# The last gate/up pair interleaved with slim quartets, and every down-projection operand loaded as a split pair

## The chip, the cores and the metric

One core of a Trainium2 chip runs the kernel. The metric is the device time of one execution in microseconds; lower is better. Everything is computed in fp32. TensorE takes fp32 matrices only in a rounded form, so each operand is split into a high and a low part, and one block product costs three matmuls of 128x128 weights on 320 columns.

## The reference, cut to what matters

One step of a hybrid encoder layer on 640 tokens (512 of a prompt, 8 times 16 of decoding). The change touches only the feed-forward part, with `D_MODEL` 2048 and `D_FF` 5632:

```python
def merge_and_ffn(x, oa, ob, ...):
    o = jnp.concatenate([rmsnorm(oa, norm_grp_a), rmsnorm(ob, norm_grp_b)], axis=-1)
    x = x + o @ w_out
    h = rmsnorm(x, norm_ffn)
    return x + (jax.nn.silu(h @ w_gate) * (h @ w_up)) @ w_down
```

## The kernel before

**Stages.** Input projection, attention and decoding run until about 700 us, the output projection until about 857 us, then come 22 feed-forward *pairs* (of 2 times 128 rows of `w_gate` and of `w_up`) until about 1949 us, then 32 steps of the down-projection until about 2500 us, and a final norm.

**Quartets.** A 2x2 block product is done with seven products instead of eight (`quartet`, L764): p1, p6, p7, p2, p5, p4, p3, each on a sum or difference of weight blocks b11, b12, b21, b22 and of operand blocks. In a pair the gate quartet (7 products of 24 matmuls) runs, then the up quartet. A quartet of a down-projection step has 7 products of 3 matmuls for each active pair: five active pairs make 105 matmuls.

- The weight combinations: `b12 -= b22` (L797) and `s6 = b11 - b12` (L801) on VectorE, `b11 = b22 - s6` (L804) and `b21 -= s6` (L813) on GpSimd. In the gate quartet of pair 0 VectorE does the last two as well (L809, L813).
- `split` (L226, L227) makes the high part of a weight block on ScalarE and the low part on VectorE. Three products' worth of split slots (H) exist.
- The partial products are added from PSUM on VectorE (L823).

**Between gate/up and down.** `store_part` (L1168) splits one of the seven operand parts of a finished pair (ScalarE, then VectorE at L1176) and stores the two halves to DRAM (`act_d`). `START` says at which down-projection step a pair enters; pairs 0 to 4 are active in step 0. An operand is fetched split by `fetch` (L1109), a 320 KB load that GpSimd's queue issues (L1112). GpSimd works in order: a load that waits for its slot holds what stands behind it. Pairs 1, 2 and 3 (`raw_pairs`) are an exception: their parts are stored whole (`first_d`, L1240), loaded by SP as the normalized inputs `hs` come free (`free`, L1118), and split on chip by `split_raws` (L1140: ScalarE L1148 21 times, VectorE L1149 14 times, GpSimd L1149 7 times). Pair 21, the last, is never stored: its parts stay in SBUF, and `keep_last` (L1154: ScalarE L1159, VectorE and GpSimd L1160) splits them during step 0; it enters in step 1.

**The order.** The program is written in one order, and a scheduler then places each engine's instructions; `keep_turns` (L143) adds dependencies that keep the tiles of one slot in the order in which they were taken, so a slot that is taken elsewhere can move instructions of other work. Work put in `n.later` stands behind the other work on ScalarE, VectorE and GpSimd. `prepare` (L1048) makes the operand parts of `hs` in pair 0's gate quartet, one set ahead of each product (L1070 to L1075, with their own splits at L226 and L227).

Of the kernel before, what the change touches and what calls it, by code (L numbers as in the profile page):

```python
# [8 lines left out]
ALU = mybir.AluOpType  # L9
# [21 lines left out]
START = [25, 27, 28, 30, 31, 3, 4, 6, 7, 8, 9, 11, 12, 14, 15, 16, 17, 19, 20, 22, 23, 1]  # L31
# [288 lines left out]
def build(nc, tc, io, pools):  # L320
# [442 lines left out]

    def quartet(k, load, lefts, before=None, after=None, part="all", eng=nc.gpsimd):  # L764

        def product(src, which, bank):
            own = n.get("H"), n.get("H")
            hl = [r(sh(x, k, P)) for x in own]
            at = n.emitted()
            n.split(sh(src, k, P), *hl)  # L770
            n.last_split = at, n.emitted()
            if before:
                before(which)
            for j in range(k):
                n.mm3(bank, (hl[0][:, j], hl[1][:, j]), lefts[j][which][1], j == 0, j == k - 1)
            n.put("H", *own)
            if after:
                after(which)
            return bank
# [8 lines left out]
        if part == "late":  # L788
            b21, b22 = get(2), get(3)
            for name, src, which in (("p2", b21, 4), ("p3", b22, 6)):  # L790
                yield name, product(src, which, n.bank()[:, :HT])
                n.put("W", src)
            return
# [17 lines left out]
        if part == "all":  # L811
            yield "p2", product(b21, 4, n.bank()[:, :HT])
        eng.tensor_tensor(b21[:, w], b21[:, w], s6[:, w], sub)  # L813
        n.put("W", s6)
        yield "p5", product(b11, 3, x[:, 1])
        n.put("W", b11)
        yield "p4", product(b21, 5, n.bank()[:, :HT])
        n.put("W", b21)
        if part == "all":
            yield "p3", product(b22, 6, y[:, 1])  # L820
        n.put("W", b22)

# [197 lines left out]
    first_d = dram("first_d", (7, P, 3, HT))  # L1020
# [94 lines left out]
    raw_pairs = active(0)[1:4]  # L1115
    raws, late, kept, kept_own = [], [], {}, []

    def free(which):  # L1118

        n.put("S", *(h[which][0] for h in hs))  # L1120
        own = []
        for j in raw_pairs[::2]:
            k = min(2, raw_pairs[-1] + 1 - j)
            raw = n.get("S")
            dma(out=sh(raw, k, HT), in_=first_d[which, :, j - raw_pairs[0]:j - raw_pairs[0] + k])
            own.append((j, k, raw))
# [12 lines left out]

    def split_raws():  # L1140
        at = n.emitted()
        which, own = raws.pop(0)
        for j, k, raw in own:
            for a in range(k):
                t = n.get("S")
                hi, lo = hl = pack(t, HT)
                part = raw[:, a * HT:a * HT + HT]
                nc.scalar.activation(hi, part, AF.Identity)  # L1148
                (nc.vector, nc.gpsimd)[a].tensor_tensor(lo, part, f(hi), ALU.subtract)  # L1149
                lefts[j + a][which] = t, hl  # L1150
            n.put("S", raw)
        n.later.append((at, n.emitted()))
# [28 lines left out]
    gate = None  # L1181
    for i in range(NPAIR):
        for src in ("w_gate", "w_up"):
            blocks = [(2 * i, 0), (2 * i + 1, 0), (2 * i, 8), (2 * i + 1, 8)]
            load = lambda z: io[src][blocks[z][0], :, blocks[z][1]:blocks[z][1] + 8]
            y = [n.get("S")]
            c11, c21 = y[0][:, :HT], y[0][:, HT:]
            start, end = i == 0 and src == "w_gate", i == NPAIR - 1 and src == "w_up"
            for step, bank in quartet(8, load, hs, (lambda w: next(prep)) if start else None, free if end else None,
                                      eng=nc.vector if start else nc.gpsimd):  # L1190
                if step == "p1":
                    nc.scalar.activation(c11, bank, AF.Identity)
                elif step == "p6":
                    y.append(n.get("S"))
                    c12, c22 = y[1][:, :HT], y[1][:, HT:]
                    add(c12, c11, bank)
                elif step == "p7":
                    add(c21, c12, bank)
                elif step == "p5":
                    add(c22, c21, bank)  # L1200
                    add(c12, c12, bank)
                elif step == "p2":
                    add(c11, c11, bank)
                elif step == "p4":
# [255 lines left out]
```

## Time and profile before

| what | value |
|---|---|
| median of 3 runs | 2529.17 us (2527.81 to 2533.78) |
| the profiled execution: its own time, its span | 2528.33 us, 2526.6 us |
| TensorE (PE) busy | 2484.5 us, 98% of the span |
| VectorE (DVE) busy | 1965.5 us, 78% |
| ScalarE (ACT) busy | 1055.0 us, 42% |
| GpSimd (POOL) busy | 701.9 us, 28% |
| the chain that ended last | PE 88%, DVE 7%, issue 2%, DMA 2%, ACT 1% |

A matmul counts as busy until its modelled end, so a busy PE can still be late; what PE loses is seen better by counting matmuls in a stretch. A busy VectorE counts the time in which it is held up by GpSimd, too. The profiled execution was 1.7 us longer than its span, and 0.8 us below the median.

### The profile page before, as it was taken

To read this page: it belongs to the slowest core of one execution; us is meant where nothing else is said; L and a number is where in the kernel's file an instruction comes from. 1 tells how busy PE (TensorE), PEld (TensorE's weight loads), DVE (VectorE), ACT (ScalarE), POOL (GpSimd) and SP (SyncE) were. 2 spreads that over 40 slices of the span, in tenths; PEclk is the share of its full clock that TensorE was granted. 3 is DMA by queue.
4 is the path that set the end of the run, shared out by engine and by line. 5 is a ranking of instruction groups with operands and counts; after the bars stand their busy time and mean duration, and the time that the engine had idled before them with its cause. 6 is when DMAs were issued, how large, how long until landed. Compare 5 with 4: busy or idle time off the path is not lost.

```text
span 2526.6 us, 44669 instructions
## 1 busy us (share of the span) xinstructions
PE 2484.5 (98%) x17325; PEld 2420.7 (96%) x17325; DVE 1965.5 (78%) x2930; ACT 1055.0 (42%) x1701; POOL 701.9 (28%) x566
## 2 busy tenths in 40 slices
PE   8999999999999999999999999999999999999997
PEld 8998999987799999999999999999999999999997
DVE  6657766685668887788888888888889877777797
ACT  5446333365555543343343343434434333333343
POOL 1001212110022043323333232333325433333453
PEclk9999999999999999999999999999999999999998
DMA  6233433478664434543344334334437756666655
GB/s 198 83 97 119 163 132 119 147 248 292 229 201 145 148 112 147 166 148 121 124 145 136 128 129 150 120 123 146 132 127 259 234 167 177 176 170 178 181 161 183
DMA packets 191605, 401.68 MB, mean 159 GB/s; under 512 B 22497, under 2 KB 83937, under 8 KB 191393
## 3 DMA queue, kind: packets, MB, share of 16 engines
q1 hardware_dynamic: 167056, 344.75, 41.8%
q0 software_dynamic: 23184, 52.77, 7.6%
q8 instruction: 136, 2.23, 0.4%
q10 hardware_dynamic: 1152, 1.31, 0.2%
q14 instruction: 77, 0.62, 0.1%
HBM read 311.14 MB, written 86.87 MB: 158 GB/s over the span
## 4 chain that ended last, share of the span: by engine, by line
PE 88%; DVE 7%; issue 2%; DMA 2%; ACT 1%; SPq 0%; POOL 0%; DVEq 0%; ACTq 0%; POOLq 0%
PE dn L235 18%; PE dn L237 18%; PE dn L236 17%; PE at L235 10%; PE at L237 10%; PE at L236 10%; DVE W L227 2%; PE at L341 2%; PE at L464 1%; PE at L425 1%; DVE S L823 1%; DMA W<-w_in 1%; PE at L743 0%; DMA W<-xT 0%; ACT S L438 0%
## 5 line engine op out<-in xcount | busy, mean ns | idle before, releaser
L226 ACT ACTIVATE W<-W 128x1024 fp32r<-128x1024 f32 (+2 forms) x662 | 640.3, 968 | 1064.3 <-PE dn L236 582.4
L235 PE MATMUL dn<-S,W 128*128 128x320 f32 x3374 | 1054.5, 313 | 7.4 <-ACT S L1159 3.8
L237 PE MATMUL dn<-S,W 128*128 128x320 f32 x3374 | 1045.8, 310 | 5.7 <-DVE W L227 5.4
L236 PE MATMUL dn<-S,W 128*128 128x320 f32 x3374 | 1044.2, 309 | 0.3 <-DVE S L227 0.3
L227 DVE TENSOR_TENSOR W<-W,W 128x1024 fp32r<-128x1024 f32 (+2 forms) x662 | 800.3, 1209 | 90.5 <-ACT W L226 83.2
L235 PEld LDWEIGHTS dn<-S,W 128*128 128x128 f32 x3374 | 634.3, 188 | 22.3 <-issue 13.5
L237 PEld LDWEIGHTS dn<-S,W 128*128 128x128 f32 x3374 | 633.6, 188 | 11.6 <-DVE W L227 9.9
L236 PEld LDWEIGHTS dn<-S,W 128*128 128x128 f32 x3374 | 634.4, 188 | 0.8 <-DVE S L227 0.6
L237 PE MATMUL at<-S,W 128*128 128x320 f32 x1834 | 567.8, 310 | 1.0 <-DVE W L227 1.0
L235 PE MATMUL at<-S,W 128*128 128x320 f32 x1834 | 567.9, 310 | 0.5 <-ACT W L226 0.5
L236 PE MATMUL at<-S,W 128*128 128x320 f32 x1834 | 567.7, 310 | 0.0
L804 POOL TENSOR_TENSOR W<-W,W 128x1024 f32<-128x1024 f32 (+2 forms) x84 | 181.4, 2159 | 772.9 <-DVE W L227 629.1
L237 PEld LDWEIGHTS at<-S,W 128*128 128x128 f32 x1834 | 345.1, 188 | 1.7 <-DVE W L227 1.4
L235 PEld LDWEIGHTS at<-S,W 128*128 128x128 f32 x1834 | 345.1, 188 | 0.7 <-ACT W L226 0.7
L236 PEld LDWEIGHTS at<-S,W 128*128 128x128 f32 x1834 | 345.1, 188 | 0.0
L823 DVE TENSOR_TENSOR S<-S,dn 128x320 f32<-128x320 f32 x398 | 182.5, 482 | 80.0 <-PE dn L237 79.7
L813 POOL TENSOR_TENSOR W<-W,W 128x1024 f32<-128x1024 f32 (+2 forms) x84 | 186.1, 2216 | 183.7 <-DVE W L227 132.8
L823 DVE TENSOR_TENSOR S<-S,at 128x320 f32<-128x320 f32 x292 | 138.6, 484 | 96.5 <-PE at L237 94.8
L797 DVE TENSOR_TENSOR W<-W,W 128x1024 f32<-128x1024 f32 (+2 forms) x86 | 117.4, 1365 | 40.8 <-DMA W<-w_gate 29.4
L801 DVE TENSOR_TENSOR W<-W,W 128x1024 f32<-128x1024 f32 (+2 forms) x86 | 95.9, 1115 | 55.1 <-DMA W<-w_up 29.6
L1112 POOL DMA_DIRECT2D S<-act_d x161 | 88.0, 547 | 166.5 <-PE dn L237 80.0
L1176 DVE TENSOR_TENSOR S<-S,half 128x320 fp32r<-128x320 f32 x147 | 120.3, 839 | 1.9
(157 smaller groups left out, 1700.4 us busy)
## 6 DMA issues: line engine op xcount, KB each, us to landing
S<-act_d POOLq DMA_DIRECT2D x161, 320.0 KB, 3.8
W<-w_gate SPq DMA_DIRECT2D x88, 512.0 KB
W<-w_up SPq DMA_DIRECT2D x88, 512.0 KB
W<-w_in SPq DMA_DIRECT2D x66, 512.0 KB
W<-w_down SPq DMA_DIRECT2D x64, 384.0 KB
act_d<-half SPq DMA_DIRECT2D x147, 160.0 KB
act_d<-S SPq DMA_DIRECT2D x147, 160.0 KB
W<-w_down SPq DMA_DIRECT2D x68, 320.0 KB
```

What stands on the lines that cost most here:

```text
L226: self.nc.scalar.activation(hi, src, AF.Identity)
L227: self.nc.vector.tensor_tensor(lo, src, f(hi), ALU.subtract)
L235: mm(out, a[0], b[0], start=first, stop=False)
L236: mm(out, a[0], b[1], start=False, stop=False)
L237: mm(out, a[1], b[0], start=False, stop=last)
L797: nc.vector.tensor_tensor(b12[:, w], b12[:, w], b22[:, w], sub)
L801: nc.vector.tensor_tensor(s6[:, w], b11[:, w], b12[:, w], sub)
L804: eng.tensor_tensor(b11[:, w], b22[:, w], s6[:, w], sub)
L813: eng.tensor_tensor(b21[:, w], b21[:, w], s6[:, w], sub)
L823: add = lambda o, a, b: nc.vector.tensor_tensor(o, a, b, ALU.add)
L1112: nc.gpsimd.dma_start(out=r(sh(t, 2, HT)), in_=r(act_d[which, :, j]))
L1176: nc.vector.tensor_tensor(r(src), src, hi, ALU.subtract)
```

## The change

- **The last pair.** `product` is taken out of `quartet`, and `slim_quartet` does the same seven products in the order p1, p7, p6, p5, p3, p2, p4 with three weight slots instead of four (b12 is worked on in place). `slim_collect` adds up the results with single PSUM tiles (one VectorE add more in each quartet). Gate and up of pair 21 run product by product in turns, 14 products, so the seven `free` calls come two products apart, over both quartets.
- **Operands.** `first_d`, `raw_pairs` and `split_raws` are gone: pairs 1 to 3 are stored by `store_part` like the others (21 ScalarE and 21 VectorE splits, 42 stores of 160 KB in place of 21), and all five pairs of step 0 are fetched from `act_d` by GpSimd: 35 loads of 320 KB instead of 14 (and SP's `first_d` loads go, 3.4 MB).
- **Pair 21** enters in step 3 instead of 1, pair 5 in step 1 instead of 3 (`START`). Its `activate` and `products` run as later work in steps 0 and 1, `keep_last` in step 2.
- `load_sums`: the loads of the residual for a step are issued one step earlier.
- The gate/up loop uses `collect` for all pairs; the first result slot is therefore taken when p1 is done and no longer ahead of the quartet.

```diff
-START = [25, 27, 28, 30, 31, 3, 4, 6, 7, 8, 9, 11, 12, 14, 15, 16, 17, 19, 20, 22, 23, 1]
+START = [25, 27, 28, 30, 31, 1, 4, 6, 7, 8, 9, 11, 12, 14, 15, 16, 17, 19, 20, 22, 23, 3]
...
+    def slim_quartet(k, load, lefts, after=None):
...
+        b11, b12, b22 = get(0), get(1), get(3)
+        nc.vector.tensor_tensor(b12[:, w], b12[:, w], b22[:, w], sub)
+        yield "p1", multiply(b11, 0)
+        yield "p7", multiply(b12, 2)
+        nc.vector.tensor_tensor(b12[:, w], b11[:, w], b12[:, w], sub)
+        nc.gpsimd.tensor_tensor(b11[:, w], b22[:, w], b12[:, w], sub)
+        yield "p6", multiply(b12, 1)
+        yield "p5", multiply(b11, 3)
+        n.put("W", b11)
+        b21 = get(2)
+        yield "p3", multiply(b22, 6)
+        n.put("W", b22)
+        yield "p2", multiply(b21, 4)
+        nc.gpsimd.tensor_tensor(b21[:, w], b21[:, w], b12[:, w], sub)
+        n.put("W", b12)
+        yield "p4", multiply(b21, 5)
+        n.put("W", b21)
...
     def free(which):
 
         n.put("S", *(h[which][0] for h in hs))
-        own = []
-        for j in raw_pairs[::2]:
...
         fetch_late()
-        raws.append((which, own))
         late.append(which)
-        if len(raws) > 2:
-            split_raws()
 
     def fetch_late():
         for which in late:
             for j in active(0):
-                if j not in raw_pairs:
-                    fetch(j, which)
+                fetch(j, which)
         late.clear()
...
-            y = [n.get("S")]
-            c11, c21 = y[0][:, :HT], y[0][:, HT:]
...
+    both = [slim_collect(slim_quartet(8, weights_of(NPAIR - 1, src), hs, after))
+            for src, after in (("w_gate", None), ("w_up", free))]
+    ys = [None, None]
+    for z in range(14):
+        ys[z % 2] = next(both[z % 2])
+        if z and z % 2 == 0:
+            store_part()
...
             if t == 0:
                 fetch_late()
-                if which in (1, 2):
-                    split_raws()
+            if (t == 0 and which in (2, 3)) or (t == 1 and which in (0, 2, 3)):
+                at = n.emitted()
+                next(finish_last, None)
+                n.later.append((at, n.emitted()))
+            elif t == 2:
                 for x in {0: (0,), 2: (1,), 4: (2,), 3: (4,), 5: (3,), 6: (5, 6)}.get(which, ()):
                     keep_last(x)
...
-        if t < 8:
-            x, y = n.get("S"), n.get("S")
...
+        if t == 0:
+            load_sums(0)
...
+                if t < 7:
+                    load_sums(t + 1)
```

GpSimd at the start of the down-projection, before. L804 and L813 are the weight combinations of step 0, L1149 and L1160 splits of operand parts, L1112 the fetches, L1231 and L1233 parts of pair 21's products:

```order
L804 TENSOR_TENSOR W_3036_20719<-W_3035_20717,W_3037_20722 128x640
L1149 TENSOR_TENSOR S_3046_20775<-S_3013_20638,S_3046_20775 128x320
L1231 TENSOR_TENSOR S_2930_20121<-S_2962_20381 128x320
L1112 DMA S_3139_21292<-act_d 128x640
L1112 DMA S_3113_21160<-act_d 128x640
L1149 TENSOR_TENSOR S_3052_20805<-S_3022_20684,S_3052_20805 128x320
L1112 DMA S_3128_21255<-act_d 128x640
L1112 DMA S_3146_21339<-act_d 128x640
L1233 TENSOR_TENSOR S_2941_20191<-S_2979_20463,S_2941_20191 128x320
L1160 TENSOR_TENSOR S_3054_20811<-S_2941_20191,S_3054_20811 128x320
L1112 DMA S_3151_21365<-act_d 128x640
L813 TENSOR_TENSOR W_3055_20816<-W_3055_20816,W_3037_20722 128x640
```

The same place after (L806 and L815 are now the combinations of step 0, L1142 the fetches, L1190 the end of the silu of pair 21):

```order
L1142 DMA S_3048_20762<-act_d 128x640
L806 TENSOR_TENSOR W_3027_20652<-W_3026_20650,W_3028_20655 128x640
L1142 DMA S_3051_20788<-act_d 128x640
L1142 DMA S_3055_20812<-act_d 128x640
L1142 DMA S_3058_20834<-act_d 128x640
L1142 DMA S_3067_20868<-act_d 128x640
L1142 DMA S_3070_20892<-act_d 128x640
L815 TENSOR_TENSOR W_3044_20740<-W_3044_20740,W_3028_20655 128x640
L1190 TENSOR_TENSOR S_2936_20135<-S_2936_20135,S_1716_9931 128x640
L1142 DMA S_3134_21272<-act_d 128x640
L1190 TENSOR_TENSOR S_2959_20281<-S_2959_20281,S_1716_9931 128x640
```

Between step 0's two combinations the splits and the products of pair 21 are gone, and five of the 35 fetches stand there.

VectorE in pair 0's gate quartet, before: W_1682 and W_1689 are the low parts for p6 and p7, the 320-wide L227 rows splits of `hs` parts, L1070 to L1073 their sums:

```order
L227 TENSOR_TENSOR W_1682_9684<-W_1670_9632,W_1681_9683 128x1024
L303 TENSOR_TENSOR S_850_5563<-S_850_5563,S_1663_9618 128x640
L1073 TENSOR_TENSOR W_1673_9638<-W_1673_9638 128x320
L227 TENSOR_TENSOR S_1697_9778<-W_1674_9639,S_1697_9778 128x320
L227 TENSOR_TENSOR W_1689_9730<-W_1667_9625,W_1688_9729 128x1024
L1070 TENSOR_TENSOR S_1677_9646<-S_1655_9550,S_1662_9614 128x320
```

The same stretch after, from p6's low part to p7's (12 rows of it; the piece ends one row ahead of W_1689):

```order
L303 TENSOR_TENSOR S_850_5562<-S_850_5562,S_1663_9617 128x640
L1103 TENSOR_TENSOR W_1674_9640<-W_1674_9640 128x320
L227 TENSOR_TENSOR S_1698_9780<-W_1675_9641,S_1698_9780 128x320
L227 TENSOR_TENSOR S_1677_9647<-W_1672_9636,S_1677_9647 128x320
L227 TENSOR_TENSOR S_1691_9737<-W_1674_9640,S_1691_9737 128x320
L1103 TENSOR_TENSOR W_1672_9636<-W_1672_9636 128x320
L1100 TENSOR_TENSOR S_1676_9644<-S_1655_9549,S_1662_9613 128x320
L227 TENSOR_TENSOR S_1699_9783<-S_1662_9613,S_1699_9783 128x320
L1101 TENSOR_TENSOR S_1676_9644<-S_1676_9644,S_1655_9549 128x320
L227 TENSOR_TENSOR S_1690_9733<-W_1672_9636,S_1690_9733 128x320
L1103 TENSOR_TENSOR S_1655_9549<-S_1655_9549 128x320
L227 TENSOR_TENSOR S_1702_9816<-W_1672_9636,S_1702_9816 128x320
```

Eleven 320-wide instructions now stand between the L303 row and p7's low part, where two stood.

SP in the same quartet, before: the load of b21 (W_1693) waits until p7's low part has freed its slot:

```order
L1095 DMA x_d<-S_1662_9614 128x640
L783 DMA W_1693_9771<-w_gate 128x1024
L783 DMA W_1738_10067<-w_up 128x1024
L783 DMA W_1727_9970<-w_up 128x1024
L783 DMA W_1726_9968<-w_up 128x1024
```

And after:

```order
L1125 DMA x_d<-S_1662_9613 128x640
L785 DMA W_1738_10066<-w_up 128x1024
L785 DMA W_1693_9770<-w_gate 128x1024
L785 DMA W_1726_9968<-w_up 128x1024
L785 DMA W_1752_10201<-w_gate 128x1024
```

A load for the up quartet now goes out ahead of the load of b21.

## Rows read from the trace of the kernel before

**Rows 1.** Stretches: busy PE, PEld, DVE, ACT, POOL (count), PEclk, DMA share, GB/s
```profile
900.00:1940.00 1040.00, 1040.00 (x7093) 1040.00 (x7092) 869.70 (x950) 417.74 (x539) 346.11 (x183) 1.00 0.42 139
1756.80:1806.00 49.20, 49.20 (x337) 49.20 (x337) 41.60 (x46) 19.54 (x26) 15.96 (x8) 1.00 0.41 133
1940.00:1980.00 40.00, 33.73 (x210) 32.05 (x210) 38.99 (x53) 15.05 (x30) 24.82 (x31) 0.96 1.03 355
1956.00:1972.00 16.00, 14.66 (x88) 14.09 (x86) 16.00 (x22) 4.30 (x9) 11.44 (x16) 0.89 1.12 394
1980.00:2011.00 31.00, 31.00 (x213) 31.00 (x213) 24.23 (x37) 11.02 (x16) 8.94 (x9) 1.00 0.62 181
2400.00:2450.00 50.00, 49.59 (x338) 49.24 (x337) 49.67 (x70) 22.48 (x33) 27.00 (x26) 1.00 0.64 176
```

**Rows 2.** What PE waited for from 1940 to 1980 us: total, times, longest
```profile
PE dn L235 <- ACT S L1159: 3.8, 1, 3.8
PE at L237 <- DVE W L227: 1.0, 1, 1.0
PE dn L235 <- ACT W L226: 0.8, 2, 0.7
PE dn L237 <- DVE W L227: 0.7, 2, 0.4
```

**Rows 3.** Timeline of ACT around that wait: start, length, idle before and its releaser
```profile
1951.63 0.47 ACT L1159 ACTIVATE S<-S 128x320 fp32r<-128x320 f32 x1 [1.16 <-DVE S L1226]
...
1954.66 0.46 ACT L1159 ACTIVATE S<-S 128x320 fp32r<-128x320 f32 x1
```

**Rows 4.** DVE and POOL by form, 1928 to 1972 us: count, busy, mean ns, idle
```profile
L1149 DVE TENSOR_TENSOR S<-S,S 128x320 fp32r<-128x320 f32 x14 | 14.3, 1047 | 0.0
...
L1112 POOL DMA_DIRECT2D S<-act_d x27 | 14.9, 555 | 7.0 <-ACT S L1159 1.7 <-issue 1.5 <-DVE S L1160 1.4
```

**Rows 5.** DMA from 1940 to 1980 us: rate by 1 us slices, POOL's queue, SP's queue, fetches
```profile
GB/s 382 405 378 389 396 376 393 375 389 389 394 389 392 392 394 392 394 405 394 399 397 397 389 397 397 392 376 405 402 348 397 407 399 389 356 152 59 56 261 26
...
q0 software_dynamic: 3269, 7.42, 54.7%
q1 hardware_dynamic: 3186, 6.76, 48.1%
...
S<-act_d POOLq DMA_DIRECT2D x18, 320.0 KB, 7.6
```

**Rows 6.** DVE and POOL by form from 2400 to 2450 us
```profile
L227 DVE TENSOR_TENSOR W<-W,W 128x640 fp32r<-128x640 f32 x21 | 26.4, 1256 | 0.2
L823 DVE TENSOR_TENSOR S<-S,S 128x320 f32<-128x320 f32 x11 | 8.4, 792 | 0.1
...
L303 POOL TENSOR_TENSOR S<-S,S 128x640 f32<-128x640 f32 x6 | 10.1, 1682 | 0.1
...
L804 POOL TENSOR_TENSOR W<-W,W 128x640 f32<-128x640 f32 x3 | 4.7, 1579 | 11.6 <-DVE W L227 11.6
L813 POOL TENSOR_TENSOR W<-W,W 128x640 f32<-128x640 f32 x3 | 4.7, 1577 | 0.6 <-DVE W L227 0.6
```

**Rows 7.** DVE by form from 1980 to 2011 us
```profile
L227 DVE TENSOR_TENSOR W<-W,W 128x640 fp32r<-128x640 f32 x15 | 14.7, 979 | 3.7 <-ACT W L226 3.2
```

**Rows 8.** Timeline of DVE in pair 0's gate quartet
```profile
863.56 0.83 DVE L303 TENSOR_TENSOR S<-S,S 128x640 f32<-128x640 f32 x1
864.30 0.49 DVE L1073 TENSOR_TENSOR W<-W 128x320 f32<-128x320 f32 x1
...
865.10 1.23 DVE L227 TENSOR_TENSOR W<-W,W 128x1024 fp32r<-128x1024 f32 x1
```

**Rows 9.** Timelines of SP, ACT and PE there: b21's load, its split, p4
```profile
866.36 0.33 SPq L783 DMA_DIRECT2D W<-w_gate  x1
...
870.12 2.01 ACT L226 ACTIVATE W<-W 128x1024 fp32r<-128x1024 f32 x2 [1.27 <-DMA W<-w_gate]
...
879.04 0.31 PE L235 MATMUL at<-S,W 128*128 128x320 f32 x1
```

More of the change, by code (lines that the diff above doesn't have):

```diff
@@ L761, in decode_a, with product @@
         n.put("W", *three)
-    def quartet(k, load, lefts, before=None, after=None, part="all", eng=nc.gpsimd):
[L766 to L779, printed above, removed]
+    def product(k, lefts, before, after, src, which, bank):
+        own = n.get("H"), n.get("H")
+        hl = [r(sh(x, k, P)) for x in own]
+        at = n.emitted()
+        n.split(sh(src, k, P), *hl)
+        n.last_split = at, n.emitted()
+        if before:
+            before(which)
+        for j in range(k):
+            n.mm3(bank, (hl[0][:, j], hl[1][:, j]), lefts[j][which][1], j == 0, j == k - 1)
+        n.put("H", *own)
+        if after:
+            after(which)
+        return bank
+    def quartet(k, load, lefts, before=None, after=None, part="all", eng=nc.gpsimd):
+        multiply = lambda *args: product(k, lefts, before, after, *args)
         def get(i):
@@ L790, in quartet @@
             for name, src, which in (("p2", b21, 4), ("p3", b22, 6)):
[L791 removed]
+                yield name, multiply(src, which, n.bank()[:, :HT])
                 n.put("W", src)
@@ new lines, in weights_of, with whole @@
+    def weights_of(i, src):
+        blocks = [(2 * i, 0), (2 * i + 1, 0), (2 * i, 8), (2 * i + 1, 8)]
+        return lambda z: io[src][blocks[z][0], :, blocks[z][1]:blocks[z][1] + 8]
+    def whole(i, src, before=None, eng=nc.gpsimd):
+        for step, y in collect(quartet(8, weights_of(i, src), hs, before, eng=eng)):
+            if step != "p1":
+                store_part()
+        return y
+    for i in range(NPAIR - 1):
+        gate = whole(i, "w_gate", (lambda w: next(prep)) if i == 0 else None, nc.vector if i == 0 else nc.gpsimd)
+        if i == 0:
+            for _ in prep:
+                pass
+            for _ in range(2):
+                n.lists["H"].append(n.lists["W"].pop())
+            r_f = n.get("S")
+            n.rstd(ssq, D, r_f)
+            n.put("S", ssq)
+        for _ in activate(gate):
+            pass
+        for _ in products(i, whole(i, "w_up"), gate):
+            pass
+        store_part()
@@ new lines, in build, with last_pair @@
+    both = [slim_collect(slim_quartet(8, weights_of(NPAIR - 1, src), hs, after))
[4 more added lines that the diff above has]
+        if z and z % 2 == 0:
+            store_part()
+    for steps in both:
+        next(steps, None)
+    def last_pair():
+        gate, y = ys
+        yield from activate(gate)
+        n.put("S", r_f)
+        yield from products(NPAIR - 1, y, gate)
+        kept.update((x[1], x[2]) for x in parts)
+        kept_own.extend(y + gate)
+        parts.clear()
```

157 lines of the change are left out of this document (66 added, 91 removed).

## The prediction

> **What bounds the kernel now.** I read the busy shares first (PE 98% of the span), then the stretches, to see where the other 2% lie. Over most of the program PE cannot go faster: from 900 to 1940 us it runs 7093 matmuls in 1040 us, 0.1466 us each, with no idle time, and the down-projection is as dense from 1980 to 2011 us [rows 1]. Between the two, from 1940 to 1980 us, stand 210 matmuls, which need 210 x 0.1466 = 30.8 us. They take 40.0. So **9.2 us** are lost there, 0.36% of the profiled execution's 2528.33 us, and no edit of this passage can win more. I then read what PE waited for in it: once 3.8 us for ScalarE's L1159, and 1.0, 0.8 and 0.7 us for weight splits [rows 2]. The timeline of ScalarE explains the long wait: the L1159 of pair 21 sits idle 1.16 us for VectorE's L1226, and the weight split that PE needs is behind it in the queue [rows 3]. After that gap the granted clock is 0.89 on average from 1956 to 1972 us, that is, some of this stretch runs at 1.2 instead of 2.4 GHz: 0.11 x 16 = 1.8 us [rows 1]. The rest are smaller gaps and late starts. Behind all of it VectorE is the engine that is full: 38.99 of 40 us, and 16.00 of 16 [rows 1], with 14 splits L1149 that take 1.05 us each [rows 4] while GpSimd works beside them. One 320-wide operation by itself takes 0.40 us from start to start, a 640-wide one 0.74 [rows 8].
>
> **Part 1: the passage is emptied (-9.2 us, and what stays).** Removed from VectorE between 1928 and 1972 us: 14 splits L1149, 14.3 us [rows 4]; keep_last is moved from step 0 to step 2, and pair 21's L1159 no longer stands ahead of step 0's splits. If nothing new came, all 9.2 us would be won. What is new:
>
> *VectorE in steps 0 to 2.* A step of 105 matmuls lasts 105 x 0.1466 = 15.4 us. By the order of after, step 0 has 11 operations of 640 columns and 9 of 320: 11 x 0.74 + 9 x 0.40 = 11.7 us. Beside it GpSimd does L806 and L815 at 1.58 us and two L1190 at about 1.7 us (as L303, the same size [rows 6]), 6.5 us. How much of this VectorE loses is read from two stretches. From 1980 to 2011 us 15 splits take 0.98 instead of 0.82 us, 2.4 us lost beside 4 combinations of 1.58 = 6.3 us: 0.4 of them [rows 7]. From 2400 to 2450 us 21 splits lose 21 x 0.44 = 9.2 us and 11 additions 11 x 0.31 = 3.4 us beside 10.1 + 4.7 + 4.7 = 19.5 us: 0.65 [rows 6]. With 0.65 step 0 needs 11.7 + 4.2 = 15.9 us, step 1 (11 and 11 operations, 5.5 us of GpSimd) 16.1, step 2 (9 and 13, 6.0 us) 15.8: 47.8 us in 46.2, short by 1.6. Three products' worth of split slots let VectorE be ahead by up to two products of 2.2 us, and where it was as full (49.67 of 50 us from 2400 to 2450) PE lost only 0.4 us [rows 1]. The ends are 0 (with 0.4) and 5 us (with all of it: 54.1 - 46.2 - 2.9, the lead less one split and its wait); I take 0.7, since the full stretch is the nearest.
>
> *GpSimd's queue of fetches.* Step 0's L815 makes b21 for its sixth product. It now stands behind five fetches, and GpSimd waits for each of them until an earlier one has landed (the order with its waits shows that eight are in flight at most). The last of these waits for the 34th of the fetches, which begin one product into the last pair. From there to L815's latest moment are 51 us (the rest of the pair, 45.7 us of 49.3, and some 5 us into step 0 with a split's lead): 1.50 us a fetch. 34 fetches of 0.328 MB are 11.1 MB; beside them go two weight blocks of pair 21 (1.0 MB), two steps' w_down (2.6), two steps' residuals (1.3) and pair 20's stores (2.3), and by the next loads' start up to 20 MB in all. At the 390 GB/s of the full slices [rows 5] 18.3 to 20 MB take 47 to 51 us: just in time. The lower bound is no stall. The upper bound is the rate that GpSimd's queue had beside a busy SP queue, 7.42 MB in 40 us, 1.77 us a fetch [rows 5]: 34 x 1.77 = 60.2, a stall of 9 us. I take 1.3 us, since SP's share is smaller here than the half it had there.
>
> The fetches' issue itself is 0.555 us while VectorE is full [rows 4]; 21 more of them are 11.7 us of GpSimd time, spread over a pair in which GpSimd is busy 15.96 of 49.2 us [rows 1], so at nothing. The Trainium skill (SBUF — State Buffer, "SBUF: two separate sides") speaks against this: a VectorE operation with two SBUF inputs and a GpSimd operation exclude each other for a whole instruction, and during VectorE's two-port modes GpSimd cannot write the descriptors of its own loads. By that rule each issue could be held for a whole VectorE operation. The row above shows the splits held up by GpSimd's arithmetic but the issues hardly, so the sum keeps 0.555. On the rate, the skill (DMA: Bandwidth & Descriptors, "Where 436 GB/s comes from") lets memory give some 358 GB/s to a core; by it the 20 MB would take 56 us, 5 us too late, an estimate from that page. This trace shows 389 to 397 GB/s for whole stretches, and the sum goes by these.
>
> So of the 9.2 us about 2.0 stay: **-7.2 us**.
>
> **Part 2: pair 0's gate quartet (a side effect).** The order of after shows nothing new in this quartet, but another sequence on VectorE: since the first result slot is taken later, slots turn differently, and between the L303 and the low part of p7 stand eleven 320-wide operations instead of two. 9 x 0.40 = 3.6 us: the low part starts at 868.7 instead of 865.10 [rows 8]. VectorE has no idle time there, so nothing absorbs it. The low part also frees the slot for b21's load: it was issued at 866.36 and the split on ScalarE started at 870.12, 3.8 us later, having waited for it [rows 9]; now it goes out at about 869.9, after a w_up load, and the split comes at 874 to 875. I followed VectorE's rows of after with these durations: p7's low part ready at 869.9, p5's at 875.8, p2's at 877.0, p4's at 880.9. PE then does 3 x 24 matmuls less the few that it could do earlier: p7 from 869.9 to 873.4, a wait until 875.8, p5 and p2 (44 matmuls, 6.5 us) until 882.25, where p4 started at 879.04 before [rows 9]. That is 3.2 us late. A wait of 0.5 us for the row norm later in the quartet then goes, since VectorE comes to it in time. Net **+2.7 us**. Bounds: +1.5 if ScalarE's parts let VectorE come to p5's split a product earlier, +4.5 if the two loads share the bandwidth and b21 lands a microsecond and more later. The small splits that moved ahead are all needed before the up quartet, so the work is only exchanged, but PE cannot regain time.
>
> **Part 3: at nothing.** Pairs 1 to 3 now do in pairs 2 to 4 what the other pairs already do: in such a stretch VectorE is busy 41.6 of 49.2 us and PE 49.2 of 49.2 [rows 1]; if that cover were gone, it would be 21 x 0.48 = 10 us. The last pair keeps its 336 matmuls, its combinations and two additions more of 0.48 us on an engine with 7.6 us to spare; all its weight blocks but two are loaded before it starts, and these two a product ahead. The earlier residual loads move bytes, not work. START and the norm at the end change no count.
>
> **Sum.** -9.2 + 2.0 + 2.7 = -4.5 us: the profiled 2528.33 become 2523.8, and, since that execution was 0.84 us below the median, **2524.6** as a median.
>
> **Rivals.**
> - *The whole gain stays* (no stall in steps 0 to 2, pair 0 costs 1.5 or less): -7.7 to -9.2, 2520.0 to 2521.5. For it: the full stretch at 2400 us, and that VectorE in pair 0 may reorder its waits for the better. Against: eleven rows for two are plain in the order.
> - *The queue of fetches takes the place of the splits:* a stall of 5 to 9 us at step 0's p4, by the 1.77 us a fetch of [rows 5], and with a gap of over 3.8 us the clock's 1.8 us come back. -9.2 + 1.8 + 5 to 9 + 2.7: 2529.5 to 2533.5, no change that can be told.
> - *Slower:* the same mechanism past its point. With q0 under 0.175 MB/us, 1.87 us a fetch, the stall is 12.6 us and the sum +7.9 (2537.1); at 160 GB/s 18.3 us and 2542.8. The measured 185 GB/s lie only just above that point, but in a passage where SP moved as much.
> - *It does not do what it says:* the order shows the five fetches, the missing L1149 and the interleaved pair, so this gets nothing.
>
> **How the numbers follow.** About 0.3% (7.6 us) is what a measurement of this kernel can tell from no change, so "faster" is below 2521.6 and "slower" above 2536.8. My forecast, 2521.6 to 2529, gets 0.52; the whole gain 0.23; the queue's stall, 2529 to 2536.8, 0.15; slower 0.10. Faster 0.23, same 0.67, slower 0.10. The range takes in most of the whole gain and of the stall: 2519.8 to 2532.5.
>
> **What would show it.** Right: from the last pair on no L1159 in PE's waits, no stretch below clock 1.0 between 1900 and 2000 us, at most 2 us of waits in steps 0 to 2, and near 868 to 876 us two new waits of PE, for p7's low part and for p5's, with p4 starting about 3 us later. Wrong: PE waiting for a split behind L815, with fetches landing 1.6 us or more apart (the queue); waits for L227 in each of steps 0 to 2 (VectorE's sum with all of GpSimd's time); pair 0's p4 at 879 (part 2 wrong). A gap in the last pair itself would mean that three slots are too few, which I hold at nothing.

## The result and the profile after

The changed kernel took **2538.52 us** as a median (2535.72 to 2540.45, 6 runs) against 2528.53 us (2527.73 to 2534.23, 6 runs) of the kernel before. The ratio is 1.0034, 95% interval 1.0024 to 1.0045: it is slower, by some 8.6 us as the ratio has it (the medians are 10.0 us apart), where 4.5 us less had been forecast. The profiled execution took 2535.72 us, its span is 2534.0 us (before: 2528.33 and 2526.6).

TensorE runs the same matmuls in the same order up to the down-projection's first steps, so its lateness can be read by comparing the start of one and the same matmul in both traces. It is 0 at 857 us; nearly all of what follows comes in four places, and from step 3 on it is +6.9 us (the spans are 7.4 us apart):

| stretch | later (+) or earlier (-) | forecast |
|---|---|---|
| pair 0's gate quartet (861 to 896 us) | +3.8 | +2.7 |
| the last pair (1914 to 1950 us) | +3.4 | 0 |
| the end of the pair and step 0 (before: 1943 to 1971 us) | -7.4 | the whole passage, 1940 to 1980 us: |
| the start of step 1 (before: 1971 to 1979 us) | +6.8 | -9.2 + 2.0 |
| steps 2 to 31 | +0.3 | 0 |
| sum | **+6.9** | -4.5 |

The stretches of after show the last three places at once. Columns are as in [rows 1]: the stretch, its length, busy PE, PEld, DVE, ACT and POOL with counts, granted clock, DMA share, GB/s.

```profile
900.00:1905.00 1005.00, 1005.00 (x6854) 1005.00 (x6854) 843.31 (x915) 398.20 (x509) 322.19 (x163) 1.00 0.40 132
1905.00:1940.00 35.00, 33.88 (x229) 33.35 (x228) 30.50 (x34) 13.25 (x18) 21.22 (x27) 1.00 0.81 253
1940.00:1972.00 32.00, 30.32 (x206) 29.85 (x204) 21.03 (x24) 9.13 (x13) 22.19 (x27) 1.00 1.15 393
1972.00:1980.00 8.00, 2.18 (x8) 1.98 (x8) 4.71 (x7) 2.10 (x3) 1.44 (x1) 0.80 0.89 328
1980.00:1988.00 8.00, 8.00 (x45) 7.92 (x45) 7.08 (x11) 2.47 (x4) 3.03 (x4) 0.78 0.44 119
1988.00:2011.00 23.00, 23.00 (x159) 23.00 (x159) 22.05 (x34) 10.32 (x19) 11.02 (x12) 1.00 0.64 186
2400.00:2450.00 50.00, 49.64 (x339) 49.40 (x338) 48.43 (x69) 23.55 (x34) 26.64 (x27) 1.00 0.62 171
```

From 1940 to 1972 us VectorE is busy 21 of 32 us: it was full there before [rows 1]. That part of the change works. But from 1972 to 1980 us PE does 8 matmuls instead of 54, and the 45 of the next 8 us stand for the lower clock. What PE waited for from 1900 to 2020 us (total, times, longest):

```profile
PE dn L235 <- ACT W L226: 5.8, 1, 5.8
PE at L237 <- DVE W L227: 2.8, 3, 1.7
```

The L1159 of [rows 2, 3] is gone, and a longer wait stands in its place, in another step. The chain of waits that ended last leads back from it (start, length, what):

```profile
1963.82 1.60 POOL W L815
1965.44 10.58 DMA W<-w_down
1976.11 0.84 DVE W L803
1977.05 0.74 ACT W L226
1977.88 0.61 PE dn L235
1978.48 0.27 PE dn L236
```

The load of step 1's b11 goes into the slot that L815 of step 0 frees, at 1965.44, and takes 10.6 us to land. ScalarE's split of b11 and VectorE's L803 both wait for it. The last row shows what follows the gap: a matmul start every 0.27 us instead of every 0.15, the 1.2 instead of the 2.4 GHz level.

The pieces of pair 0's quartet that answer to [rows 8, 9], from the timelines of VectorE, SP, ScalarE and PE of after: L303 and p7's low part; b21's load; its split (with p5's); p4's start.

```profile
863.27 0.82 DVE L303 TENSOR_TENSOR S<-S,S 128x640 f32<-128x640 f32 x1
...
868.42 1.22 DVE L227 TENSOR_TENSOR W<-W,W 128x1024 fp32r<-128x1024 f32 x1
...
869.67 0.33 SPq L785 DMA_DIRECT2D W<-w_gate  x1
...
873.38 2.22 ACT L226 ACTIVATE W<-W 128x1024 fp32r<-128x1024 f32 x2 [3.98 <-PE at L236]
...
875.65 0.41 PE L235 MATMUL at<-S,W 128*128 128x320 f32 x1 [0.60 <-ACT W L226]
...
882.50 0.31 PE L235 MATMUL at<-S,W 128*128 128x320 f32 x1
```

The low part stood at 865.10 and p4 at 879.04 before. And the last pair, from the timelines of VectorE, GpSimd and ScalarE:

```profile
1908.60 1.21 DVE L840 TENSOR_TENSOR W<-W,W 128x1024 f32<-128x1024 f32 x1
1912.76 4.96 DVE L840 TENSOR_TENSOR W<-W,W 128x1024 f32<-128x1024 f32 x1
1918.78 2.69 DVE L1181 TENSOR_TENSOR S<-S,half 128x320 fp32r<-128x320 f32 x1
1945.64 3.95 DVE L227 TENSOR_TENSOR W<-W,W 128x1024 fp32r<-128x1024 f32 x1 [4.49 <-ACT W L226]
...
1914.18 2.45 POOL L841 TENSOR_TENSOR W<-W,W 128x1024 f32<-128x1024 f32 x1
1917.85 3.27 POOL L841 TENSOR_TENSOR W<-W,W 128x1024 f32<-128x1024 f32 x1 [1.23 <-issue]
1941.56 0.53 POOL L1142 DMA_DIRECT2D S<-act_d  x1 [0.39 <-DVE S L854]
1942.11 2.41 POOL L849 TENSOR_TENSOR W<-W,W 128x1024 f32<-128x1024 f32 x1
1946.08 2.42 POOL L849 TENSOR_TENSOR W<-W,W 128x1024 f32<-128x1024 f32 x1
...
1944.55 1.06 ACT L226 ACTIVATE W<-W 128x1024 fp32r<-128x1024 f32 x1 [6.49 <-POOL W L849]
```

One and the same subtraction (L840) lasts 1.21 us at 1908.60 and 4.96 us at 1912.76, beside GpSimd's L841; a split (L1181, 0.48 us by itself) lasts 2.69 beside the second L841; L849 stands behind seven fetches from 1932.84 to 1941.56 that each wait for an earlier landing, then makes ScalarE wait 6.49 us, and the split that follows it (L227) lasts 3.95 instead of 1.21 us beside the second L849. PE's three gaps, from one matmul's start to the next, are 1.06, 0.68 and 1.99 us long, right behind these.

### The profile page after: what moved, and what is told of

Read it like the earlier page. It is cut to its first block, busy times and chain, and to the rows that moved or that the text cites. A ratio compares the mean times of both kernels' runs of the same rounds, so it can differ in the third digit from the quotient of the medians.

```text
span 2534.0 us, 44565 instructions
## 1 busy us (share of the span) xinstructions
PE 2485.5 (98%) x17325; PEld 2421.3 (96%) x17325; DVE 1963.4 (77%) x2918; ACT 1047.1 (41%) x1680; POOL 703.4 (28%) x580
## 4 chain that ended last, share of the span: by engine, by line
PE 86%; DVE 7%; DMA 3%; issue 2%; ACT 1%; POOL 0%; SPq 0%; DVEq 0%; ACTq 0%; POOLq 0%
PE dn L235 17%; PE dn L237 17%; PE dn L236 17%; PE at L235 10%; PE at L237 10%; PE at L236 10%; DVE W L227 2%; PE at L341 2%; PE at L464 1%; PE at L425 1%; DMA W<-w_in 1%; DVE S L854 1%; DMA W<-w_down 1%; DMA W<-w_gate 1%; PE at L743 0%
## 5 line engine op out<-in xcount | busy, mean ns | idle before, releaser
L235 PE MATMUL dn<-S,W 128*128 128x320 f32 x3310 | 1037.3, 313 | 9.2 <-ACT W L226 8.3
L237 PE MATMUL dn<-S,W 128*128 128x320 f32 x3310 | 1028.6, 311 | 7.4 <-DVE W L227 7.0
L236 PE MATMUL dn<-S,W 128*128 128x320 f32 x3310 | 1026.5, 310 | 0.0
L227 DVE TENSOR_TENSOR W<-W,W 128x1024 fp32r<-128x1024 f32 (+2 forms) x662 | 802.2, 1212 | 89.7 <-ACT W L226 82.7
L235 PEld LDWEIGHTS dn<-S,W 128*128 128x128 f32 x3310 | 623.8, 188 | 23.7 <-issue 13.7
L237 PEld LDWEIGHTS dn<-S,W 128*128 128x128 f32 x3310 | 622.8, 188 | 13.5 <-DVE W L227 11.7
L236 PEld LDWEIGHTS dn<-S,W 128*128 128x128 f32 x3310 | 623.7, 188 | 0.2 <-issue 0.2
L237 PE MATMUL at<-S,W 128*128 128x320 f32 x1898 | 588.5, 310 | 3.4 <-DVE W L227 3.4
L235 PE MATMUL at<-S,W 128*128 128x320 f32 x1898 | 588.4, 310 | 1.2 <-ACT W L226 1.2
L236 PE MATMUL at<-S,W 128*128 128x320 f32 x1898 | 587.9, 310 | 0.0
L806 POOL TENSOR_TENSOR W<-W,W 128x1024 f32<-128x1024 f32 (+2 forms) x82 | 176.1, 2148 | 756.9 <-DVE W L227 567.9
L237 PEld LDWEIGHTS at<-S,W 128*128 128x128 f32 x1898 | 357.0, 188 | 4.9 <-DVE W L227 4.6
L235 PEld LDWEIGHTS at<-S,W 128*128 128x128 f32 x1898 | 357.2, 188 | 1.7 <-ACT W L226 1.7
L236 PEld LDWEIGHTS at<-S,W 128*128 128x128 f32 x1898 | 357.1, 188 | 0.0
L854 DVE TENSOR_TENSOR S<-S,dn 128x320 f32<-128x320 f32 x390 | 178.6, 481 | 76.5 <-PE dn L237 75.4
L815 POOL TENSOR_TENSOR W<-W,W 128x1024 f32<-128x1024 f32 (+2 forms) x82 | 180.6, 2203 | 176.9 <-DVE W L227 124.5
L854 DVE TENSOR_TENSOR S<-S,at 128x320 f32<-128x320 f32 x302 | 143.0, 483 | 96.8 <-PE at L237 95.7
L1142 POOL DMA_DIRECT2D S<-act_d x182 | 99.0, 546 | 178.3 <-PE dn L237 83.6
L799 DVE TENSOR_TENSOR W<-W,W 128x1024 f32<-128x1024 f32 (+2 forms) x84 | 111.3, 1325 | 41.8 <-DMA W<-w_gate 27.2
L803 DVE TENSOR_TENSOR W<-W,W 128x1024 f32<-128x1024 f32 (+2 forms) x84 | 92.2, 1097 | 60.0 <-DMA W<-w_up 32.3
L1181 DVE TENSOR_TENSOR S<-S,half 128x320 fp32r<-128x320 f32 x147 | 128.4, 895 | 2.1
```

The source lines that it names most:

```text
L227: self.nc.vector.tensor_tensor(lo, src, f(hi), ALU.subtract)
L235: mm(out, a[0], b[0], start=first, stop=False)
L236: mm(out, a[0], b[1], start=False, stop=False)
L237: mm(out, a[1], b[0], start=False, stop=last)
L799: nc.vector.tensor_tensor(b12[:, w], b12[:, w], b22[:, w], sub)
L803: nc.vector.tensor_tensor(s6[:, w], b11[:, w], b12[:, w], sub)
```

## The experiments

Ratios are against the kernel before, run beside each on the same chip, with 95% intervals. "Late" is TensorE's start of the same matmul against before at about 2011 us, less the same difference at 857 us: up to there, ahead of the feed-forward part, the profiled executions already lie from 1.2 us ahead of to 5.1 us behind that of before. It is +6.9 us for the changed kernel. Each value is read from one execution.

**Pair 0: is the slot the cause, and is it given back?** *a_early* is the changed kernel with the first result slot taken ahead of the quartet again:

```diff
-    def collect(steps):
+    def collect(steps, y=()):
-        y = []
+        y = list(y)
...
-                y.append(n.get("S"))
+                if not y:
+                    y.append(n.get("S"))
...
-        for step, y in collect(quartet(8, weights_of(i, src), hs, before, eng=eng)):
+        for step, y in collect(quartet(8, weights_of(i, src), hs, before, eng=eng), [n.get("S")]):
```

> The changed kernel with one thing undone: the first result slot of each gate/up quartet is taken ahead of the quartet again. By the order of instructions pair 0's gate quartet is then as in the kernel before on every engine, and the rest as in the changed kernel. Theory: the late slot costs what the starts of PE show between pair 0 and the last pair, 3.8 us, so 3.8 us less than the changed kernel (2538.5 to about 2534.7), with p4 of pair 0's gate at 879.2 us instead of 882.6. Rival: the loss is given back later (the down-projection waits for its loads until the DMA backlog is gone, whenever PE arrives), and the time stays within 1 us of the changed kernel, the stall in step 1 being longer by what pair 0 wins.

Measured: 2533.52 us, ratio 1.0015 (1.0006 to 1.0025). Pair 0 is -0.25 us against before instead of +3.8; late at the end +2.2. The gap in step 1 stays, 5.75 us. The loss of pair 0 is not given back later.

*b_late* is the other way round: the kernel before, with nothing changed but the slot, taken at p1.

```diff
-            y = [n.get("S")]
-            c11, c21 = y[0][:, :HT], y[0][:, HT:]
+            y = []
...
                 if step == "p1":
+                    y.append(n.get("S"))
+                    c11, c21 = y[0][:, :HT], y[0][:, HT:]
```

> The kernel before with that one thing alone: the first result slot is taken when p1 is done. Theory: 3.8 us more than the kernel before (2528.5 to about 2532.3), all of it between 857 and 900 us; the passage from 1940 to 1980 us is shifted but loses the same 9.2 us. Rival: part of the 3.8 us is won back in that passage, since the loads there get ahead; then 1 to 2 us more than before.

Measured: 2534.6 us, ratio 1.0015 (1.0005 to 1.0024). Pair 0 +4.4 us, and +4.9 at the end; the passage from 1940 to 1980 us is as before (L1159 3.9 us). The place of one allocation costs 4 to 5 us in the kernel before and in the changed one.

**The last pair: three slots, or GpSimd?** *a_vecp* keeps the three slots and the order of products, and gives the four combinations of the pair to VectorE.

```diff
-        nc.gpsimd.tensor_tensor(b11[:, w], b22[:, w], b12[:, w], sub)
+        nc.vector.tensor_tensor(b11[:, w], b22[:, w], b12[:, w], sub)
...
-        nc.gpsimd.tensor_tensor(b21[:, w], b21[:, w], b12[:, w], sub)
+        nc.vector.tensor_tensor(b21[:, w], b21[:, w], b12[:, w], sub)
```

> The changed kernel with the last pair's four weight combinations on VectorE instead of GpSimd. Theory: the three gaps of PE in the last pair (0.9, 0.5 and 1.8 us at 1918, 1922 and 1948 us) go, the first two since VectorE is no longer held up by GpSimd's combinations, the third since the combination no longer stands behind fetches: 3 us less in the pair, of which the stall in step 1 may take some back (b11's load is still behind the fetches). Rival: VectorE is held up by GpSimd's issuing of fetches too (one b12 combination of 1.14 us took 4.96 us beside four issues and one combination), so the first two gaps stay at 0.5 us or more and only the third goes.

Measured: 2534.7 us, ratio 1.0013 (1.0004 to 1.0023); late +2.0. PE has no wait at all from 1900 to 1950 us; one of 1.3 us comes in step 0 instead. The same place on VectorE and GpSimd:

```profile
1919.12 1.23 DVE L840 TENSOR_TENSOR W<-W,W 128x1024 f32<-128x1024 f32 x1
...
1917.15 4.28 POOL L1142 DMA_DIRECT2D S<-act_d  x8
```

Of the eight fetches issued from 1917.15 us on, 0.535 us each, two to three fall beside that L840, which still lasts 1.23 us. So issues alone did not hold VectorE here, the gaps go with GpSimd's arithmetic, and the three slots are enough. (Of the 4.96 us after, L841 covers 2.45 and the subtraction itself 1.2; the first 1.3 us, beside the fetches issued ahead of L841, stay unexplained.) The gap in step 1 is 3.6 us here.

**Step 1: GpSimd's queue?** *a_vec0* gives step 0's two combinations to VectorE, so that nothing of step 0 stands behind the fetches and the slot of step 1's b11 no longer waits for L815 on GpSimd. (Where VectorE makes it, `b11 = b22 - s6` also stands two products later, behind p7.)

```diff
-                                  nc.vector if t == STEPS - 1 else nc.gpsimd):
+                                  nc.vector if t in (0, STEPS - 1) else nc.gpsimd):
```

> The changed kernel with step 0's two weight combinations (b11 = b22 - s6, b21 -= s6) on VectorE instead of GpSimd. Nothing else moves but what follows from it on VectorE and GpSimd. Theory (queue): the 5.8 us wait of PE in step 1 comes from the second combination standing behind five fetches on GpSimd, since the load of step 1's b11 takes its slot; on VectorE it is done about 3 to 4 us sooner, so the load is issued at about 1961.5 instead of 1965.4 us, the wait falls to 2 or 3 us, the clock is not halved any more (2.2 us), and the time is 5 to 6 us below the changed kernel. Rival (bytes): the load lands when the DMA backlog is through, at about 1974 us, whenever it is issued: the wait stays above 4 us and the time within 1.5 us of the changed kernel.

Measured: 2538.32 us, ratio 1.0031 (1.0021 to 1.004), late +7.9; the gap in step 1 is 6.8 us long and ends at 1982.68. The earlier load that the expectation counted on did not come about: SP stood at a residual load, and b11's load (the second of the last row) went out at about 1968 us instead of 1965.44.

```profile
1954.69 10.79 SPq L1293 DMA_DIRECT2D S<-x_d  x2
...
1967.47 0.85 SPq L785 DMA_DIRECT2D W<-w_down  x2
```

So the gap does not need GpSimd's queue; what an earlier load of b11 would do, this run does not show.

**The bytes?** *a_half* fetches only the high part of each of step 0's 35 operands and takes it for the low part too; the low part is left out:

```diff
-                fetch(j, which)
+                t = n.get("S")
+                hi = r(t[:, :HT])
+                nc.gpsimd.dma_start(out=hi, in_=r(act_d[which, :, j, 0]))
+                lefts[j][which] = t, (hi, hi)
```

> The changed kernel with each of step 0's 35 fetches halved to 160 KB: only the high part is loaded and used in place of the low part too, so the output is not the reference's. Every instruction and every wait stays, 5.7 MB of traffic go (14.7 us at 390 GB/s). Theory (bytes): the DMA is no longer full after about 1955 us, fetches and weight loads land in 4 to 6 us, PE's wait in step 1 and the one of 1.7 us at the end of the last pair go: 7 to 9 us below the changed kernel. Rival (waits of the queues by themselves): SP and GpSimd still stand behind slots that PE frees late, and more than 3 us of the wait in step 1 stay.

Measured: 2527.68 us, ratio 0.9992 (0.9983 to 1.0001), late -1.9, with pair 0's loss still in it. The gap of step 1 shrinks to 1.3 us. So the bytes count (or GpSimd's waits for their landing, which shrink with them).

**The order on SP?** *a_defer* puts the residual loads of steps 1 to 7 behind the loads of b12 and b22 of their own step.

```diff
+                if 0 < t < 8:
+                    at = n.emitted()
+                    load_sums(t)
+                    n.loads.append(((begun, at), (at, n.emitted())))
...
-                if t < 7:
-                    load_sums(t + 1)
...
+    n.keep_loads()
```

> The changed kernel with SP's order changed in one thing: the residual loads of steps 1 to 7 stand behind their own step's loads of b12 and b22 instead of ahead of them. In the changed kernel SP stands still from 1950.5 to 1960.0 us at the residual load of step 2, whose slot is freed only when a store of pair 20 has landed, with step 1's weight loads behind it, and four residual loads go out among them while the DMA is full. Theory (SP's queue): the weight loads of step 1 go out up to 9 us earlier and 1.3 MB (3.4 us at 390 GB/s) less lie ahead of them; the 5.8 us wait in step 1 falls below 2.5 us and the clock is not halved: 5 to 7 us below the changed kernel. Rival (the load of b11): that load still waits for step 0's combination behind the fetches, at about 1965 us, and lands some 8 to 10 us later; the wait stays above 4 us and the time within 2 us of the changed kernel.

Measured: 2530.5 us, ratio 1.0009 (1.0000 to 1.0018), late +2.1. PE's wait for the weight split is gone; what stays from 1900 to 2020 us:

```profile
PE at L248 <- DVE W L238: 2.4, 2, 2.0
PE dn L246 <- DVE S L865: 1.4, 1, 1.4
```

(L238 is L227, L865 is L854 and L1208 is L1197 with the inserted lines.) The first is the last pair's. The second is VectorE's own lateness in step 1, behind a product of pair 21 that takes 2.03 us instead of 0.81, beside a GpSimd combination from 1975.12 to 1976.69 us:

```profile
1975.34 2.03 DVE L1208 TENSOR_TENSOR S<-S,S 128x640 f32<-128x640 f32 x1
1977.29 0.81 DVE L238 TENSOR_TENSOR W<-W,W 128x640 fp32r<-128x640 f32 x1
1978.03 0.47 DVE L865 TENSOR_TENSOR S<-S,dn 128x320 f32<-128x320 f32 x1
```

*a_sums* undoes only the edit that draws the residual loads one step forward.

```diff
-        if t == 0:
-            load_sums(0)
+        if t < 8:
+            load_sums(q)
...
-                if t < 7:
-                    load_sums(t + 1)
```

> The changed kernel with one edit: the residual loads (load_sums) are issued in the step that adds them, as in the kernel before, and no longer one step ahead. Theory A (SP's order: the residual load that was drawn forward stands in SP's queue ahead of step 1's weight loads, waits for its slot, and so makes them late): the gap of 6.1 us in step 1 goes, as with the residual loads put behind the step's weight loads; TensorE ends 4 to 6 us earlier than in the changed kernel, about +1 to +3 us against before, ratio 1.0005 to 1.0012. Theory B (the residual loads are late for any placing ahead of the weight loads, since their slots are freed by stores that crawl through the full queues): the weight loads of step 1 now wait behind step 1's own residual loads; the gap of step 1 stays over 3 us, ratio 1.002 to 1.0035.

Measured: 2536.05 us, ratio 1.0023 (1.0013 to 1.0034), late +3.7. The gap of 6 us is gone, two of 1.2 and 1.8 us stay, the last pair loses 4.8 instead of 3.4: the gap goes as theory A had it, the ratio is in the range of theory B. Its step 1 is repaired (+1.3 us there instead of +6.8); 1.4 us more are lost in the last pair, and 0.7 us less are won behind it.

What the residual loads do is read from SP's longest wait (the first row), SP's queue and ScalarE's split of b11. After, one residual load (the second L1293 of the third row) waits 9.0 us for its slot, which a store of operand parts frees, and b12, b22 and more residual loads stand behind it and then go out together, ahead of b11 (the second of the last SP row, 1965.44):

```profile
SPq L1293 <- DMA act_d<-S: 9.0, 1, 9.0
...
1950.05 0.38 SPq L1183 DMA_DIRECT2D act_d<-S  x1
1950.52 9.82 SPq L1293 DMA_DIRECT2D S<-x_d  x2
1960.40 0.42 SPq L785 DMA_DIRECT2D W<-w_down  x1
1960.91 0.86 SPq L1292 DMA_DIRECT2D S<-x_d  x2
1961.86 0.38 SPq L1293 DMA_DIRECT2D S<-x_d  x1
1962.34 3.43 SPq L785 DMA_DIRECT2D W<-w_down  x2
...
1976.12 0.74 ACT L226 ACTIVATE W<-W 128x640 fp32r<-128x640 f32 x1 [8.69 <-DMA W<-w_down]
```

and in a_defer, where b12 is out at 1952.28, b22 some 8 us later, and b11's load is the first of the third row:

```profile
1952.28 8.75 SPq L796 DMA_DIRECT2D W<-w_down  x2
1961.12 0.38 SPq L1303 DMA_DIRECT2D S<-x_d  x1
...
1965.33 4.82 SPq L796 DMA_DIRECT2D W<-w_down  x2
...
1971.50 0.74 ACT L237 ACTIVATE W<-W 128x640 fp32r<-128x640 f32 x1 [1.85 <-DMA W<-w_down]
```

The load of b11 goes out at 1965.44 and at 1965.33, the same time, and lands after 10.6 and after 6.1 us. What was issued just ahead of it differs: six loads by SP from 1960.0 to 1962.3 us after, three from 1960.7 to 1961.6 us in a_defer; that this makes the difference is argued from the order and not tested by itself. How full the DMA is shows the rate in 40 slices of 1 us, from 1950 us on: in turn after, a_vec0, a_ev (below) and a_defer.

```profile
GB/s 378 398 389 399 366 378 385 385 389 392 410 407 410 397 389 399 387 394 389 392 394 384 397 397 389 399 407 397 191 46 0 95 233 44 251 33 26 271 31 0
...
GB/s 392 392 388 379 383 384 392 402 386 357 393 388 384 390 398 410 399 410 402 397 389 394 389 394 394 387 397 387 394 410 405 405 300 70 5 0 174 154 74 251
...
GB/s 396 405 415 407 397 392 402 382 397 399 397 392 407 405 399 384 405 207 60 0 51 253 28 207 115 0 189 138 0 0 138 225 230 61 0 0 61 277 298 282
...
GB/s 384 385 388 399 392 376 378 380 398 402 415 407 405 402 399 392 392 394 405 392 389 405 348 264 379 402 347 54 238 69 87 397 371 197 243 15 0 90 271 195
```

After, the DMA runs full until 1978.5 us (28 full slices and one of 191), and PE's gap ends at 1977.88; in a_vec0 until 1982.8, the gap to 1982.68; in a_ev until 1967.5, the gap to 1967.23. In the same way it is 1975.5 and 1974.86 in a_early, 1978.9 and 1978.60 in a_vecp. **The gap of step 1 ends within 0.7 us of the end of one backlog of transfers** in all five kernels that keep the residual loads where the change put them and fetch the operands whole: step 1's weights are among the last loads of it. In a_defer the backlog is about as long (to 1977 us, thinner from 1972 us on), but step 1's weights are in by 1971.5 to 1972.6 us.

**Are the three losses separate?** *a_ev* is a_early and a_vecp together, *a_evd* has a_defer's order as well, and *a_evdv* adds a_vec0's line to that.

> The changed kernel with two of the three edits together: the result slot of a pair is taken ahead of its quartet again, and the last pair's four weight combinations run on VectorE. The residual loads stay one step ahead. If the three losses are separate terms: pair 0 is back (3.5 us won), the last pair's three gaps are gone (3.4 us won), and step 1 still waits for its weight loads, 3 to 6 us with the clock's loss behind it: end of TensorE 0 to -3 us against before, ratio 0.999 to 1.0003. If the step-1 wait comes from the other two being late (the loads' slots freed late): the wait is under 1.5 us and the ratio is 0.9978, as with all three edits.

> Three things together on the changed kernel: the result slot taken early, the last pair's combinations on VectorE, the residual loads behind their step's first weight loads. If the losses are separate: 3.6 + 5 + 5 us below the changed kernel less what two of them share in step 1's wait (about 3), so some 2528, level with the kernel before. If the b11 load behind the fetches sets step 1 whatever else is done: 5 to 6 us more than that, about 2533.

> The same three, and step 0's combinations on VectorE too, so that the load of step 1's b11 no longer waits for GpSimd's queue. If that load is what is left, the wait in step 1 falls below 1 us and the time to 2521 to 2525, below the kernel before. If the backlog of bytes is what is left, it is within 1.5 us of the run without this fourth thing.

| kernel | median, us | ratio | late, us | PE's gap in step 1, us |
|---|---|---|---|---|
| a_ev | 2526.91 | 0.9996 (0.9987 to 1.0006) | -2.5 | 4.1 |
| a_evd | 2523.99 | 0.9978 (0.9969 to 0.9987) | -7.0 | 1.7 |
| a_evdv | 2523.49 | 0.9978 (0.9969 to 0.9987) | -8.3 | 1.2 |

By lateness the single repairs give 4.7 (a_early), 5.0 (a_vecp) and 4.8 (a_defer) us. From +6.9 the first two lead to -2.8 (measured -2.5), all three to -7.6 (measured -7.0): the three repairs add up. They are not one place each: of a_vecp's 5.0 us some 3 are won in step 1, whose gap is 3.6 instead of 6.1 us there, and 1.6 are lost in step 0. a_evd is faster than both kernels, and lower than either value that its expectation named (2528 and 2533). The fourth edit moves the trace by 1.3 us and the median by nothing that can be told.

## Why the prediction was wrong

**Part 1, the emptied passage: right in kind, and most of it was won.** Up to the end of step 0 PE loses nothing: the 140 matmuls that took 28.0 us before take 20.5, 0.1467 us each. 7.4 of the 9.2 us stood there. VectorE's price in steps 0 to 2 was put at 0.7 us; outside the start of step 1 nothing is lost in them (the 0.3 us of the table's row of steps 2 to 31 are lost at 2013.8 us, in step 3). The reading of [rows 3] was loose: the two weight splits on ScalarE had ended by 1954.44, and PE's matmul at 1955.38 starts 0.26 us behind the end of L1159 and 0.10 us behind that of VectorE's addition L823, which stands behind two L1149; the trace does not tell the two apart.

**Part 1, the queue of fetches: the step that failed.** For L815 the sum came out: 18.3 to 20 MB at 390 GB/s, 47 to 51 us from the first fetch of the last pair, which would be 1959 to 1963 us from the 1912.04 of after. L815 did run at 1963.82, and step 0's p4 did not wait, so "just in time" held for the consumer that the prediction had picked, though by luck in part: from 1912 to 1964 us the DMA moved 17.7 MB at a mean of 340 GB/s, fewer bytes at a lower rate. But the backlog went on to 1978.5 us, and the first consumer behind it was another: step 1's b11, b12 and b22. The working counted two steps' weights as bytes that slow the fetches and never asked when these weights land themselves. Its term of 1.3 us measured **6.8 us** in another place: 8.7 us lost for the 35 matmuls that start it (a gap of 6.1 us less one matmul's 0.15, and 2.7 us behind it, mostly at the lower clock), against 1.9 us that the same matmuls lost before. The rival of the fetch queue had the price (5 to 9 us, with the clock's loss) but the wrong victim; the gap came without a stall of step 0's p4, and in a_vec0 without L815 on GpSimd. The measured 2538.52 us lie above the forecast's whole range, among the values that got 0.10; that the rival *slower* names a near number (2537.1) is luck, since the stall of 12.6 us that it is made of did not come. (Its other sum is slightly off: at 160 GB/s 34 fetches take 69.7 us, a stall of 18.7 and not 18.3 us.)

**Part 3, "the earlier residual loads move bytes, not work": wrong.** In a passage where the DMA is full, bytes are the work: with the residual behind the weights (a_defer) 4.8 us come back. SP's stand at a load whose slot is not free, and the bytes that go out ahead of the weights once it is, were not told apart, since both edits that move the residual (a_defer, a_sums) change both; which of the two costs how much stays open.

**Part 3, the last pair at nothing: wrong by 3.4 us.** Its 7.6 us of VectorE's slack were an average over a pair. With the quartets interleaved, L840 of up meets L841 of gate, and L849 waits behind fetches in GpSimd's order; the prediction counted issue time (0.555 us each, which held) and not the wait for landings that stands between the issues. The prediction took a gap in this pair to mean that three slots are too few; a_vecp has three and no gap.

**Part 2, pair 0: the mechanism held, the size was short.** Forecast and measured: low part of p7 868.7 and 868.42, b21's load 869.9 and 869.67, p5 875.8 and 875.65, p4 882.25 and 882.50. The net is +3.8 and not +2.7: p4 starts 0.25 us later than forecast, 0.6 us more are lost behind its start, and of the 0.5 us that the wait for the row norm was to give back only 0.2 came (PE's gap there is 0.60 us, ending at 895.90, instead of 0.82).

Of the signs of being right, two came (no L1159 in PE's waits; p7 and p5 waiting in pair 0, with p4 3.5 us late), and two did not (there is a stretch at clock 0.8, and 5.8 us of waits stand in steps 0 to 2). The sign of the queue, PE waiting for a split behind L815, came in another form: the split is that of step 1's b11, whose load takes the slot that L815 frees.

The Trainium skill's rule on the shared port (SBUF — State Buffer, "SBUF: two separate sides"), by which a VectorE operation with two SBUF inputs and a GpSimd operation that reads SBUF exclude each other for a whole instruction, is what the 4.96 us and 3.95 us rows look like by their length. The order of the starts does not show it: this L840 and this L227 start 1.42 and 0.44 us ahead of GpSimd's operation and still end behind it. The prediction weighed it for the DMA issues alone, where a_vecp's row agrees with the 0.555, and not for the combinations of the last pair. The Trainium skill's some 358 GB/s to a core (DMA: Bandwidth & Descriptors, "Where 436 GB/s comes from") is lower than this trace: 27 of the 28 first slices of after stand at 378 to 410.

## What to carry to other kernels

When a change makes the DMA run full over several stages, write down every load of these stages in the order in which it is needed, and ask which consumer meets the end of the backlog: here it was the weights of the next step, not the instruction whose queue was lengthened. What is needed late (here the residual) belongs behind what is needed soon, even if it could go out earlier. And of two engines that hold each other up, slack is to be read at the instruction where they meet, not as a mean over a stage.

## What the runs showed of the hardware beyond that

- Two loads of the same 320 KB, issued at the same time of the program (1965.44 and 1965.33), took 10.6 and 6.1 us to land, both in stretches at some 390 GB/s; the fetches on GpSimd's queue took 7.6 us in the full stretch of before [rows 5].
- PE's clock fell behind the gap of 6.1 us (0.80 and 0.78 in the two stretches of 8 us after) and not behind the 1.7 us of a_evd, which end at 1969.96: the stretches from 1956 and from 1972 us have 1.00 (columns as above):

```profile
1956.00:1972.00 16.00, 14.28 (x94) 13.50 (x93) 15.96 (x20) 5.28 (x8) 9.06 (x10) 1.00 0.93 301
1972.00:1980.00 8.00, 8.00 (x56) 8.00 (x55) 7.73 (x13) 3.32 (x5) 3.88 (x3) 1.00 0.59 196
```

- Where a tile is allocated in the program, with no other difference, moved this kernel by 4 to 5 us (a_early, b_late); small instructions on VectorE, which is full there, then stand in another order.
